# RWKV-7 head pairs 0 and 1 of a block side by side in one decoder block's kernel

## The chip, the cores and the metric

The kernel runs on one core of a Trainium2 chip. The core has a matrix engine (TensorE, PE in the profile; PEld are its weight loads), two engines for elementwise work (VectorE, DVE, and ScalarE, ACT), GpSimdE (POOL) and SyncE (SP), which only issues transfers here. ScalarE issues transfers too. Each engine works through its own instructions in the order in which they were laid out when the program was built, and waits on semaphores for the others. Matrix products land in PSUM (eight banks of 512 floats per partition); all else lies in SBUF or in DRAM. The metric is the time of one execution in microseconds (us) on the device.

## What is computed

One layer of a hybrid decoder, 2048 tokens of width 1024, all in 32-bit floats:

```python
h = rmsnorm(x, norm1_g) * (1.0 + sc1) + sh1
p = h @ w_in                       # 27 column groups of 128
ya = rglru_mixer(...)              # 256 wide
yb = hgrn2_mixer(...)              # 384 wide, 6 heads of 64
yc = rwkv7_mixer(...)              # 384 wide, 6 heads of 64
y = jnp.concatenate([ya, yb, yc], axis=-1) * mix_beta
x = x + g1 * (y @ w_out)
h = rmsnorm(x, norm2_g) * (1.0 + sc2) + sh2
x = x + g2 * swiglu(h, ffn_w_gate, ffn_w_up, ffn_w_down)
return rmsnorm(x, final_g)
```

The RWKV-7 mixer shifts each input column group by one token (`ps = pc + (prev - pc) * mu`), makes a decay `w` and a gate `a` per token from low-rank products (`tanh(wl) @ w_up`, `al @ a_up`, through a sigmoid) and an output gate `g = sigmoid(gl) @ g_up`, and runs this recurrence per head with a 64x64 state:

```python
sa = einsum('bhvk,bhk->bhv', S, -kkt)
S = S * wt + sa[..., None] * (kkt * at) + vt[..., None] * kt
y_t = einsum('bhvk,bhk->bhv', S, rt)
```

After it stand a group norm per head, a bonus term and the output gate.

## The kernel before

**Tiling.** Tokens are cut into 4 blocks of 512 (`TB`, `NB`), a block into 8 chunks of 64 (`NCH`). Channels lie on the 128 partitions, so an RWKV "pair" `pr` is two heads (`e` is 0 or 1), and there are three pairs.

**Dense work.** `project` (L238 to L249) multiplies weights, split into a rounded part and a rest (`wh`, `wl`), with activations split alike (`hh`, `hl`): three matmuls of 128x128 by 128x512 for each 128x128 weight block, 9696 in all. The raw weights come in through three buffers `wr`, and each is split by ScalarE (`wh`) and VectorE (`wl`, L221) into four buffers each.

**Order of work.** The program is written as straight Python and a planner orders the instructions of each engine by priority and by its own estimate of when operands are ready. `level` (L67) sets the priority: results of dense work first ("out"), then weight loads ("load"), norms and inputs ("feed"), the mixers ("mix"), and last the dense matmuls ("dense"). So dense matmuls fill TensorE wherever no mixer instruction was expected to be ready. `w_in_products` computes the 27 column groups of `p` in the order of `IN_ORDER` (L35), for blocks 0 and 1 together and then for 2 and 3, and stores them in DRAM (`pd`). `mixers(b)` reads them; its outputs go to `yd` in DRAM. `w_out_products` and `ffn` of block b are traced after `mixers(b + 1)`; `load_y` reads `yd` for the output projection.

**The mixers of a block** (L871): `lora`, then `rwkv` for pair 0, `hgrn` 0, `rglru` 0, `rwkv` for pairs 1 and 2, `hgrn` 1, `rglru` 1, `hgrn` 2.

`lora` (L473) keeps the low-rank inputs in the tiles `l1` and `l2` for the whole block. `rwkv` (L501) does one pair, in these stages:

- Prologue: two low-rank products (`low_rank`, L486) with a sigmoid give the decay input `sc` and the gate `a`; a scan along the tokens (L513), exponentials and products give per chunk the 128x256 operand `KG` and the 128x128 operand `BK`, with two buffers each. A matmul per chunk (L553), masked on VectorE (L556, L557), gives `GIQ`, one buffer, which holds the chunk's triangular system and its output weights. `BK` is transposed (L562).
- Inverse: the 32x32 diagonal blocks go through DRAM (`nd`, L569) into `NL` and `NX`, which lie with 32 blocks per group of 32 partitions, in four groups. 30 steps of a multiplication and an addition on VectorE (L599, L601) invert them. They go back through DRAM (`xd`, L607 and L610) into `GIQ`. Eight transposes of 32x32 per half (L617) and two rounds of eight 32x32 matmuls (L621, L626) make the off-diagonal blocks.
- Values: `v`, transposed and with its mean taken off, goes into `VS` (L584).
- Recurrence: for each of 8 chunks a chain of three visits to TensorE, with VectorE and ScalarE between: L641 (and L642), copy to `rs`; L650, copy to `VS`; L653 (and L654), then the new state with the decay `we` (L658). The products lie in one PSUM bank, `pc`.
- End: norm, bonus and output gate (L669), store to `yd` (L671).

A product of 32-bit operands shows as two instructions on TensorE, so 96 chunk steps (4 blocks, 3 pairs, 8 chunks) are x192 in the views. `hgrn` (L680) has its own tiles `VS2` and `AQ`. The scratch tiles of the RWKV part are nine buffers named `tr`, those of the other mixers eight named `th`. Tiles named `pm` are three PSUM banks, `ph` one, `pd` three, `pc` one.

Of the kernel before, what the change touches and what calls it, by code (L numbers as in the profile page):

```python
# [34 lines left out]
IN_ORDER = (25, 26, 19, 16, 22, 7, 4, 10, 13, 0, 2, 20, 17, 23, 8, 5, 11, 14, 1, 3, 21, 18, 24, 9, 6, 12, 15)  # L35
# [16 lines left out]
def hybrid_kernel(ctx, tc, x, par, ada_w, w_in, rgw, igw, w_up, a_up, g_up, w_out,  # L52
# [105 lines left out]
    ones = cp.tile([128, 128], F, name="ones")  # L158
    V.memset(ones, 1.0)
# [312 lines left out]

    def lora(b):  # L473
        t = shifted(b, 9, tr_())
        act(t[0:64], t[0:64], AF.Tanh)
        t1 = [mp.tile([128, TB], R, name=f"l1{i}", bufs=1) for i in range(2)]
# [4 lines left out]
        t2 = mp.tile([128, TB], F, name="l2", bufs=1)  # L481
        shifted(b, 10, t2)
        act(t2, t2, AF.Sigmoid)
        return t1, t2

    def low_rank(i, cols, l1):  # L486
        pz = pm_()
        PE.matmul(pz, LW[i][:, cols], l1[i], start=True, stop=False)
        PE.matmul(pz, LW[2 + i][:, cols], l1[i], start=False, stop=True)
        return pz  # L490
# [7 lines left out]
    GIQ = mp.tile([128, NCH, 2, 2, 64], F, name="GIQ")  # L498
    G.memset(GIQ, 0.0)

    def rwkv(b, pr, lr):  # L501
        cols = slice(pr * 128, (pr + 1) * 128)
        l1, l2 = lr
        k = shifted(b, 3 + pr, tr_())
        pz = low_rank(0, cols, l1)
        sc = tr65_()
        V.memset(sc[:, :, 0:1], 0.0)
        act(sc[:, :, 1:65], c64(pz), AF.Sigmoid, bias=pc("w0", pr))
        pz = low_rank(1, cols, l1)
        a = tr_()  # L510
        act(a, pz, AF.Sigmoid, bias=pc("a0", pr))
        cum = tr65_()
        V.tensor_tensor_scan(cum.rearrange("p c t -> p (c t)"), d0, sc.rearrange("p c t -> p (c t)"), 0.0,  # L513
                             op0=OP.mult, op1=OP.add)
# [28 lines left out]
        we = mp.tile([128, NCH], F, name="we", bufs=2)  # L543
# [5 lines left out]
        for q in range(0, NCH, 2):  # L549
# [4 lines left out]
            for e in range(2):  # L554
                s, o = HD[e]
                V.tensor_mul(GIQ[s, q:q + 2, :, e, :], pv[s, :, :, e], gm[s, None].to_broadcast([64, 2, 2, 64]))  # L556
# [7 lines left out]


        nd = tc.dram_tile([4 * NCH, 32, 32], F, name=f"nd{b}_{pr}")
        for blk in range(4):
            b2 = blk % 2
            A.dma_start(nd[blk * NCH:(blk + 1) * NCH].rearrange("c j i -> j c i"),  # L569
                         GIQ[32 * blk:32 * blk + 32, :, 0, blk // 2, 32 * b2:32 * b2 + 32])  # L570
        v = shifted(b, 6 + pr, tr_())
        pb, _ = blocksum(r, pm_(), "tr")
        VS = mp.tile([128, NCH, 2, 64], F, name="VS", bufs=1)
# [6 lines left out]
        for e in range(2):  # L580
            s, o = HD[e]
            for par in range(2):
                t = slice(par * 64, par * 64 + 64)
                stt(VS[o, par:NCH:2, e, :], mean[t, :, e:e + 1].to_broadcast([64, NG, 64]), -1.0 / 64, p4[t, :, e, :],  # L584
                    OP.mult, OP.add)
        bonus = v
        V.tensor_mul(bonus, v, pb)
        NL = mp.tile([128, 32, 32], F, name="NL", bufs=1)
        NX = mp.tile([128, 8, 32], F, name="NX", bufs=1)
        n4 = nd.rearrange("b (m g) i -> b m g i", g=4)  # L590
        for g in range(4):
            quarter = slice(32 * g, 32 * g + 32)
            A.dma_start(NL[quarter], nd)
            A.dma_start(NX[quarter], n4[:, :, g, :])
        for j in range(1, 31):
            m, n = (j + 3) // 4, 31 - j
            tmp = mp.tile([128, 72], F, name="ftmp", bufs=1)
            tv = tmp[:, :m * n].rearrange("p (c i) -> p c i", i=n)
# [3 lines left out]
        xd = tc.dram_tile([4 * NCH, 32, 32], F, name=f"xd{b}_{pr}")  # L602
        x4 = xd.rearrange("b (m g) i -> b m g i", g=4)
        for g in range(4):
# [428 lines left out]
```

## Time and profile before

| | |
|---|---|
| median of 3 runs | 2882.71 us (2879.23 to 2887.38) |
| the profiled execution, its own time | 2884.81 us |
| its span (first to last instruction) | 2883.0 us |
| TensorE's granted clock, mean | 0.986 |
| GpSimdE busy | 81.5 us |

A row of a group of instructions reads: line, engine, operation, tile written and tiles read, shape, count; then busy time and mean duration of one in ns; then the engine's idle time just before these instructions, and what ended it. Matmuls overlap each other in the pipeline, so a matmul's listed duration (399 ns for the dense ones) is longer than the distance from its start to the next one's. A row of the table of stretches reads: from and to, length; busy time and count of TensorE's matmuls, of its weight loads, of VectorE, ScalarE and GpSimdE; granted clock; share of the DMA engines, GB/s. A row of a timeline reads: start, duration, engine, line, operation; in brackets the engine's idle time before it and what ended it. A row of waits reads: who waited for whom, us in total, times, the longest. A DMA issue's row reads: shortest, median and longest time of the issue in ns, first and last start in us.

### The profile page before, as it was taken

The page shows a single profiled execution, that of the slowest core. Times are in us where ns is not written, and L with a number is a line of the kernel's source. Part 1 is how long each engine was busy: PE and PEld are TensorE (multiplying, and loading weights), DVE is VectorE, ACT ScalarE, POOL GpSimd, SP SyncE. Part 2 cuts the span into 40 slices and gives each one's busy share as a digit, 9 for nine tenths or more (in the row PEclk, how much of TensorE's full clock was granted, in tenths as well). Part 3 has the DMA queues.
Part 4 walks back from the last instruction along what each step waited for, and adds up shares of the span by engine and source line. Part 5 has one row for each costly group of instructions (what it writes and reads, how often), then busy time and mean ns, then how long its engine had stood idle before and what let it go on. Part 6 is the DMA issues. An engine that isn't in the chain of part 4 may idle for free. (4 is left out here: it accounts for less than half of the span.)

```text
span 2883.0 us, 41762 instructions
## 1 busy us (share of the span) xinstructions
PE 2761.2 (96%) x14842; PEld 2189.4 (76%) x14842; DVE 1975.3 (69%) x4617; ACT 1500.2 (52%) x2514; POOL 81.5 (3%) x67
## 2 busy tenths in 40 slices
PE   7999999999999899999989999999999999999998
PEld 6777777777777677777767787777777888788886
DVE  8776768778586777868788777778964444644445
ACT  4528465263636737565684556757644233533323
POOL 2000000000001000000100000001000001000000
PEclk9999999999999999999999999999999999999999
DMA  7534455434344233333453233344432333433332
GB/s 255 161 103 142 137 160 182 129 121 133 98 125 142 89 88 100 103 92 100 115 160 88 84 105 101 96 114 122 122 94 88 96 99 117 146 99 96 98 96 87
DMA packets 235041, 337.52 MB, mean 117 GB/s; under 512 B 73041, under 2 KB 78673, under 8 KB 234833
## 3 DMA queue, kind: packets, MB, share of 16 engines
q1 hardware_dynamic: 160144, 285.55, 31.9%
q10 hardware_dynamic: 74688, 49.31, 6.7%
q8 instruction: 117, 1.92, 0.3%
q14 instruction: 92, 0.75, 0.1%
HBM read 286.53 MB, written 48.23 MB: 116 GB/s over the span
## 5 line engine op out<-in xcount | busy, mean ns | idle before, releaser
L248 PE MATMUL pd<-hh,wh 128*128 128x512 f32 x3232 | 1285.4, 399 | 16.6 <-ACT hh L78 14.2
L248 PE MATMUL pd<-hl,wh 128*128 128x512 f32 x3232 | 1289.3, 399 | 3.1 <-DVE hl L81 3.0
L248 PE MATMUL pd<-hh,wl 128*128 128x512 f32 x3232 | 1283.6, 397 | 0.0
L78 ACT ACTIVATE wh<-wr 128x512 fp32r<-128x512 f32 (+1 forms) x752 | 463.6, 620 | 865.3 <-PE pd L248 713.4
L221 DVE TENSOR_TENSOR wl<-wr,wh 128x512 fp32r<-128x512 f32 (+1 forms) x752 | 509.0, 681 | 315.6 <-ACT wh L78 307.7
L248 PEld LDWEIGHTS pd<-hh,wh 128*128 128x128 f32 x3232 | 611.3, 189 | 144.0 <-ACT hh L78 17.7
L248 PEld LDWEIGHTS pd<-hl,wh 128*128 128x128 f32 x3232 | 611.8, 189 | 129.1 <-DVE hl L81 7.4
L248 PEld LDWEIGHTS pd<-hh,wl 128*128 128x128 f32 x3232 | 611.9, 189 | 121.9 <-issue 2.6
L81 DVE SCALAR_TENSOR_TENSOR xs<-pd,Q,xs 128x512 f32<-128x512 f32 x224 | 167.6, 748 | 124.6 <-PE pd L248 114.5
L78 ACT ACT_TABLE_LOAD x183 | 234.8, 1283 | 12.1 <-issue 4.7
L78 ACT ACTIVATE xs<-pd 128x512 f32<-128x512 f32 x140 | 82.8, 591 | 66.0 <-PE pd L248 60.8
L78 ACT ACTIVATE th<-th 128x512 f32<-128x512 f32 (+2 forms) x153 | 93.7, 613 | 44.9 <-DVE th L787 19.7
L917 DVE TENSOR_TENSOR xs<-pd,xs 128x512 f32<-128x512 f32 x88 | 60.7, 690 | 77.0 <-PE pd L248 75.2
L78 ACT ACTIVATE hh<-xs 128x512 fp32r<-128x512 f32 x120 | 74.1, 627 | 38.1 <-DVE xs L917 25.3
L78 ACT ACTIVATE hw<-VS,we 64x64 f32<-64x64 f32 x192 | 66.0, 344 | 42.2 <-DVE VS L81 38.8
L599 DVE TENSOR_TENSOR ftmp<-NX,NL 128x30 f32<-128x30 f32 (+4 forms) x360 | 73.9, 205 | 8.6 <-issue 1.2
L601 DVE TENSOR_TENSOR NX<-NX,ftmp 128x30 f32<-128x30 f32 (+4 forms) x360 | 73.7, 205 | 7.2
L78 ACT ACTIVATE tr<-tr 128x512 f32<-128x512 f32 (+3 forms) x100 | 62.3, 626 | 16.8 <-DVE tr L81 15.0
L81 DVE SCALAR_TENSOR_TENSOR VS<-pc,we,hw 64x64 f32<-64x64 f32 x168 | 47.4, 282 | 32.7 <-PE pc L653 28.9
L217 POOL TENSOR_TENSOR hl<-xs,hh 128x512 fp32r<-128x512 f32 x32 | 46.8, 1488 | 810.4 <-ACT hh L78 571.3
L78 ACT ACTIVATE xs<-xs 128x512 f32<-128x512 f32 x77 | 47.7, 626 | 36.1 <-DVE xs L81 22.9
L221 DVE TENSOR_TENSOR hl<-xs,hh 128x512 fp32r<-128x512 f32 x88 | 61.8, 703 | 5.6 <-ACT hh L78 1.1
(234 smaller groups left out, 2665.1 us busy)
## 6 DMA issues: line engine op xcount, KB each, us to landing
wr<-in_w_gate SPq DMA_DIRECT2D x176, 256.0 KB, 2.6
wr<-in_w_upf SPq DMA_DIRECT2D x176, 256.0 KB, 2.6
wr<-in_w_down SPq DMA_DIRECT2D x160, 256.0 KB, 2.7
wr<-in_w_in SPq DMA_DIRECT2D x144, 256.0 KB, 3.3
pd<-xs SPq DMA_DIRECT2D x108, 256.0 KB, 2.9
xs<-in_x SPq DMA_DIRECT2D x72, 256.0 KB, 4.4
wr<-in_ada_w SPq DMA_DIRECT2D x64, 256.0 KB, 3.3
th<-pd ACTq DMA_DIRECT2D x64, 256.0 KB, 3.4
```

What stands on the lines that cost most here:

```text
L78: return A.activation(o, i, f, **k)
L81: return V.scalar_tensor_tensor(o, a, s, b, op0=op0, op1=op1)
L217: G.tensor_sub(lo, src, hi.bitcast(F))
L221: V.tensor_sub(lo, src, hi.bitcast(F))
L248: PE.matmul(p, a[:, c], b, start=(n == 0), stop=(n == tot - 1))
L599: V.tensor_mul(tv, NX[:, 0:m, j:j + 1].to_broadcast([128, m, n]), NL[:, j:j + 1, j + 1:32].to_broadcast([128, m, n]))
L601: V.tensor_add(NX[:, 0:m, j + 1:32], NX[:, 0:m, j + 1:32], tv)
L917: V.tensor_mul(t, pu, t)
```

## The change

- `rwkv` takes a list of pairs. `mixers` calls it for pairs 0 and 1 together and then for pair 2 alone. `rwkv_chunks` (the prologue), `invert` and `rwkv_values` are functions of their own; `GIQ`, `VS`, `pc`, `rs` and `hw` have an index `u` for the pair within the call.
- `invert` puts the diagonal blocks of both pairs on the partitions: 64 blocks per group in two groups for a joint call, 32 in four for a single one. The 30 steps are the same, with about twice the elements per partition in a joint call. The 32x32 transposes of a half and pair are one instruction on 256 columns, and the matmuls of both halves come before the copies.
- In the recurrence each of the three visits does the products of both pairs; the copies to `rs` and `VS` serve both in one instruction. The decayed state (`hw`) and the new state are still one instruction per pair and head. The third visit's product overwrites the first's place in `pc`.
- `lora` computes the low-rank products of all three pairs at once and stores `sc`, `a` and the output gate's input in DRAM (`ld`); `rwkv_chunks` loads `sc` and `a`, and the end of `rwkv` loads the gate's input for each pair.
- Two tiles named `big` (2048 floats per partition) serve `NL`, `NX` and the scratch of the steps, then `VS`, and `VS2` with `AQ` of `hgrn`, in place of tiles of their own. `rs` and `hw` have one buffer instead of two, `we` four instead of two. `ones` is a view of `aones`.
- `IN_ORDER` brings the column groups of pair 1 forward.

```diff
-IN_ORDER = (25, 26, 19, 16, 22, 7, 4, 10, 13, 0, 2, 20, 17, 23, 8, 5, 11, 14, 1, 3, 21, 18, 24, 9, 6, 12, 15)
+IN_ORDER = (25, 26, 19, 16, 20, 17, 22, 23, 7, 4, 10, 13, 0, 2, 21, 18, 24, 8, 5, 11, 14, 1, 3, 9, 6, 12, 15)
...
     def lora(b):
...
+        ld = tc.dram_tile([4, 2, 128, 520], F, name=f"ld{b}")
+        t2 = shifted(b, 10, tr_())
         act(t2, t2, AF.Sigmoid)
+        A.dma_start(ld[3, 0, :, 0:TB], t2)
+        for pr in range(3):
+            cols = slice(pr * 128, (pr + 1) * 128)
+            pz = low_rank(0, cols, t1[0])
+            sc = tr65_()
+            V.memset(sc[:, :, 0:1], 0.0)
+            act(sc[:, :, 1:65], c64(pz), AF.Sigmoid, bias=pc("w0", pr))
+            A.dma_start(ld[pr, 0], sc.rearrange("p c t -> p (c t)"))
+            pz = low_rank(1, cols, t1[1])
+            a = tr_()
+            act(a, pz, AF.Sigmoid, bias=pc("a0", pr))
+            A.dma_start(ld[pr, 1, :, 0:TB], a)
+        return ld
...
+    def big_():
+        return mp.tile([128, 2048], F, name="big", bufs=2)
+
+    def rwkv_chunks(b, u, pr, ld, nd):
         k = shifted(b, 3 + pr, tr_())
+        sc = tile_of("tr")
+        A.dma_start(sc, ld[pr, 0])
         a = tr_()
-        act(a, pz, AF.Sigmoid, bias=pc("a0", pr))
+        A.dma_start(a, ld[pr, 1, :, 0:TB])
...
+    def invert(b, prs, nd):
+        nu = len(prs)
+        nb, ng = 4 * nu * NCH, 4 // nu
+        t = big_()
+        NL = t[:, 0:1024].rearrange("p (j i) -> p j i", i=32)
+        NX = t[:, 1024:1536].rearrange("p (m i) -> p m i", i=32)
+        n4 = nd.rearrange("b (m g) i -> b m g i", g=ng)
+        for g in range(ng):
+            part = slice(nb * g, nb * g + nb)
+            A.dma_start(NL[part], nd)
+            A.dma_start(NX[part, 0:32 // ng], n4[:, :, g, :])
         for j in range(1, 31):
-            m, n = (j + 3) // 4, 31 - j
+            m, n = (j + ng - 1) // ng, 31 - j
+            tv = t[:, 1536:1536 + m * n].rearrange("p (c i) -> p c i", i=n)
             V.tensor_mul(tv, NX[:, 0:m, j:j + 1].to_broadcast([128, m, n]),
                          NL[:, j:j + 1, j + 1:32].to_broadcast([128, m, n]))
             V.tensor_add(NX[:, 0:m, j + 1:32], NX[:, 0:m, j + 1:32], tv)
...
+        for e, (lo, up) in enumerate(half):
+            for u in range(nu):
+                V.transpose(X1[lo, u * 256:u * 256 + 256], GIQ[lo, :, u, 0, e, 0:32])
+            for u in range(nu):
+                for c in range(NCH):
+                    PE.matmul(pv[up, u, c], GIQ[lo, c, u, 0, e, 32:64], xv[lo, u, c], start=True, stop=True)
...
+    def rwkv(b, prs, ld):
+        nu = len(prs)
+        nd = tc.dram_tile([4 * nu * NCH, 32, 32], F, name=f"nd{b}_{prs[0]}")
+        ops = [rwkv_chunks(b, u, pr, ld, nd) for u, pr in enumerate(prs)]
+        invert(b, prs, nd)
+        VS = big_().rearrange("p (c u e v) -> p c u e v", u=2, e=2, v=64)
+        bonus = [rwkv_values(b, u, pr, op[3], VS) for u, (pr, op) in enumerate(zip(prs, ops))]
...
+                for u, (KG, BK, we, r) in enumerate(ops):
+                    PE.matmul(pcn[:, u, 0:2, :], KG[:, c, 0].rearrange("p e t -> p (e t)"), both[u], start=True, stop=True)
+                for u, (KG, BK, we, r) in enumerate(ops):
+                    PE.matmul(py[:, c - q, u], both[u], KG[:, c, 1], start=(c == q and u == 0), stop=False,
+                              skip_group_check=True)
+                V.tensor_copy(rs[0:64, 0:nu], pcn[0:64, 0:nu, 0, :])
+                act(rs[64:128, 0:nu], pcn[64:128, 0:nu, 1, :])
+                for u, (KG, BK, we, r) in enumerate(ops):
+                    for e in range(2):
+                        s, o = HD[e]
+                        act(hw[s, u], VS[s, c, u, e, :], AF.Copy, scale=we[s, c:c + 1])
+                for u in range(nu):
+                    PE.matmul(pcn[:, u, 2, :], GIQ[:, c, u, 0].rearrange("p e t -> p (e t)"), rs[:, u], start=True,
+                              stop=True)
+                V.tensor_copy(VS[0:64, c, 0:nu, 0, :], pcn[0:64, 0:nu, 2, :])
+                act(VS[64:128, c, 0:nu, 1, :], pcn[64:128, 0:nu, 2, :])
...
-            rwkv(b, 0, lr)
+            rwkv(b, (0, 1), lr)
             hgrn(b, 0)
             rglru(b, 0)
-            rwkv(b, 1, lr)
-            rwkv(b, 2, lr)
+            rwkv(b, (2,), lr)
```

More of the change, by code (lines that the diff above doesn't have):

```diff
@@ L157, in hybrid_kernel @@
     V.memset(aones.bitcast(F), 1.0)
-    ones = cp.tile([128, 128], F, name="ones")
-    V.memset(ones, 1.0)
+    ones = aones.bitcast(F)
     epsc = cp.tile([128, 3], F, name="epsc")
@@ L471, in shifted, with low_rank @@
         return t
+    def low_rank(i, cols, l1):
+        pz = pm_()
+        PE.matmul(pz, LW[i][:, cols], l1, start=True, stop=False)
+        PE.matmul(pz, LW[2 + i][:, cols], l1, start=False, stop=True)
+        return pz
     def lora(b):
@@ L475, in lora @@
         act(t[0:64], t[0:64], AF.Tanh)
-        t1 = [mp.tile([128, TB], R, name=f"l1{i}", bufs=1) for i in range(2)]
+        t1 = [tile_of("tr", R)[:, 0:TB] for i in range(2)]
         for i in range(2):
@@ L629, in rwkv @@
[L629 to L646 removed]
+        xd = tc.dram_tile([nb, 32, 32], F, name=f"xd{b}_{prs[0]}")
@@ new lines, in invert @@
+        x4 = xd.rearrange("b (m g) i -> b m g i", g=ng)
+        for g in range(ng):
+            part = slice(nb * g, nb * g + nb)
+            V.memset(NX[part].rearrange("p m i -> p (m i)")[:, g:1024 // ng:32 + ng], 1.0)
+            A.dma_start(x4[:, :, g, :], NX[part, 0:32 // ng])
+        for u in range(nu):
+            for blk in range(4):
+                b2 = blk % 2
+                n = (4 * u + blk) * NCH
+                A.dma_start(GIQ[32 * blk:32 * blk + 32, :, u, 0, blk // 2, 32 * b2:32 * b2 + 32],
+                            xd[n:n + NCH].rearrange("c l i -> l c i"))
@@ new lines, in invert @@
+        for e, (lo, up) in enumerate(half):
+            V.tensor_copy(TT[up, 0:n], p[up, 0:n])
+        p = pm_()
+        pv = p.rearrange("p (u c t) -> p u c t", u=2, t=32)
+        for e, (lo, up) in enumerate(half):
+            for u in range(nu):
+                for c in range(NCH):
+                    PE.matmul(pv[lo, u, c], tv[up, u, c], GIQ[up, c, u, 0, e, 32:64], start=True, stop=True)
+        for e, (lo, up) in enumerate(half):
+            for u in range(nu):
+                V.tensor_copy(GIQ[lo, :, u, 0, e, 32:64], pv[lo, u])
@@ L697, in hgrn @@
         pair = th_()[:, 0:TB // 2]
-        VS = mp.tile([128, 2, NCH, 64], F, name="VS2", bufs=1)
-        AQ = mp.tile([128, 2, NCH, 64], F, name="AQ", bufs=1)
+        VS, AQ = big_().rearrange("p (two e c v) -> two p e c v", two=2, e=2, v=64)
         p = ph_()
```

162 lines of the change are left out of this document (59 added, 103 removed).

## The prediction

> **What bounds the kernel now.** I read the page first (the span, part 1), then the table of stretches, the groups of TensorE by form, the DMAs that touch yd (the finished mixer outputs), the list of waits and two stretches of the timeline.
>
> ```profile
> span 2883.0 us, 41762 instructions
> ...
> PE 2761.2 (96%) x14842; PEld 2189.4 (76%) x14842; DVE 1975.3 (69%) x4617; ACT 1500.2 (52%) x2514; POOL 81.5 (3%) x67
> ```
>
> ```profile
> 2250.00:2400.00 150.00, 150.00 (x663) 124.27 (x662) 60.69 (x90) 45.73 (x75) 0.00 (x0) 1.00 0.33 98
> ```
>
> The first fence is the page's span and part 1, the second a stretch in which no mixer work is left: 663 dense matmuls in 150 us, 226 ns each, TensorE never idle.
>
> ```profile
> L248 PE MATMUL pd<-hl,wh 128*128 128x512 f32 x3232 | 1289.3, 399 | 3.1 <-DVE hl L81 3.0
> ...
> L641 PE MATMUL pc<-VS,KG 128*128 128x128 f32 x192 | 41.9, 300 | 4.1 <-DVE VS L81 3.9
> L653 PE MATMUL pc<-VS,BK 128*128 128x128 f32 x192 | 41.6, 298 | 5.5 <-ACT VS L78 5.0
> ...
> L650 PE MATMUL pc<-rs,GIQ 128*128 128x64 f32 x192 | 36.7, 273 | 3.5 <-ACT rs L78 3.3
> ...
> L621 PE MATMUL pm<-tr,GIQ 32*32 32x32 f32 x384 | 26.7, 199 | 4.4 <-DVE tr L617 4.1
> ```
>
> The dense product is issued in three kinds of 3232 instructions (one is quoted), 9696 in all: at 226 ns they need 2191 us of the 2883. The other 692 us hold 5146 small matmuls of the mixers and norms, the time lost in going over to them and back, and 122 us (2883.0 less 2761.2) of plain idle time. So TensorE is the bound, and only what shortens this remainder moves the end. Idle time in front of the recurrence (L641, L650, L653) is 13.1 us in all, in front of the inverse's matmuls (L621) 4.4 us: what stands idle openly is small.
>
> Is the mixers' chain a second bound? Source L671 stores a finished RWKV pair; L140 loads yd for the output projection of a block (here block 3; the answer for the tile yd in the window from 2100 us).
>
> ```profile
> L671 ACTq DMA_DIRECT2D yd<-tr x12: 326/326/353, 250.2 to 2199.0; - x12
> ```
>
> ```profile
> L140 SPq DMA_DIRECT2D xs<-yd x8: 319/327/435, 2414.7 to 2428.9; - x8
> ```
>
> The last RWKV output leaves at 2199.0 us and is asked for at 2414.7: 216 us to spare. The twelve stores are 11 intervals apart, (2199.0 - 250.2) / 11 = 177 us per pair, 531 us per block. Making this chain shorter gains nothing by itself; dense matmuls fill TensorE while it waits. What counts is how often TensorE must leave the dense stream for it.
>
> **The change part by part.**
>
> *Recurrence, pairs 0 and 1 together.* Every matmul is still issued (five products per pair and chunk), but a chunk step of two pairs has the three visits to TensorE (L641 with L642, L650, L653 with L654) that one pair had. Before: 4 blocks x 3 pairs x 8 chunks x 3 = 288 visits; after: 4 x 2 x 8 x 3 = 192, 96 fewer. The price of a visit beside its own matmuls:
>
> ```profile
> 1083.68 0.39 PE L248 MATMUL pd<-hh,wh 128*128 128x512 f32 x1
> 1083.91 0.38 PE L653 MATMUL pc<-VS,BK 128*128 128x128 f32 x2
> 1084.13 0.39 PE L654 MATMUL pm<-GIQ,VS 128*128 128x128 f32 x2
> 1084.27 0.48 PE L248 MATMUL pd<-hl,wh 128*128 128x512 f32 x1
> 1084.59 0.40 PE L248 MATMUL pd<-hh,wl 128*128 128x512 f32 x1
> ```
>
> Start to start, a dense matmul takes 0.23 us, but the first one after the visit takes 0.32 (1084.27 to 1084.59): 0.09 us on the way back. On the way in, the waits view gives what the weight loads waited:
>
> ```profile
> PEld pc L653 <- ACT VS L78: 20.8, 48, 1.8
> PEld pc L650 <- ACT rs L78: 19.7, 49, 1.0
> ...
> PEld pc L641 <- issue: 11.3, 32, 2.8
> ```
>
> That is 51.8 us over 288 visits, 0.18 us each at most; the matmuls' own idle rows above (13.1 us) make 0.045 at least, since a weight load can wait while the array still works. I take the middle, near 0.09, as half of each load wait lies under the dense matmul before it. A visit costs 0.09 + 0.09 = 0.18 us, and 96 fewer save **17 us**; ends 96 x 0.135 = 13 and 96 x 0.27 = 26 us. If the schedule puts dense matmuls between the two pairs' products, the visits do not shrink in number and the saving is near 0; that is the first rival.
>
> *Inverse, pairs 0 and 1 together.* Per pair, 16 transposes of 32x32 feed 16 products; now one 32x256 transpose per pair and half, and all products of both halves stand in one row.
>
> ```profile
> 1074.80 0.37 PE L621 MATMUL pm<-tr,GIQ 32*32 32x32 f32 x6
> 1075.10 0.50 PE L248 MATMUL pd<-hh,wl 128*128 128x512 f32 x1
> 1075.53 0.37 PE L621 MATMUL pm<-tr,GIQ 32*32 32x32 f32 x6
> ```
>
> The sixteen instructions of a half (two per product) come in pieces of six with one dense matmul between, which then holds TensorE for 0.43 us instead of 0.23 (1075.10 to 1075.53). The eight transposes of a half take 0.84 us; the view of line L621 says what ended its waits:
>
> ```profile
> 1074.03 0.84 DVE L617 STREAM_TRANSPOSE tr<-GIQ 32x32 f32<-32x32 f32 x8
> ```
>
> ```profile
>   DVE tr L617: 14.7, 19
>   issue: 10.6, 41
> ```
>
> 60 waits, 25.3 us, 0.42 each, over 12 pairs. After, 8 inversions with about two such entries each, 16 in all, at the transposes' own mean of 14.7 / 19 = 0.77 us since TensorE now waits for a whole transpose: 12.4 us. Saved: **13 us**. Ends: 25 if the order of issue foresees the wide transposes, 5 if each of the 24 (two per pair) keeps TensorE for the 0.84 us of eight narrow ones (20 us), and -8 if each of the 8 inversions meets a wait of 4.1 us, the whole wait in L621's row above (33 us): a wide transpose is not in this trace. I take the middle, nearest to the mean of L621's rows.
>
> *VectorE.* The substitution takes 60 instructions per inversion, 12 x 60 before and 8 x 60 after, with twice the elements for the joint ones.
>
> ```profile
> L601 DVE TENSOR_TENSOR NX<-NX,ftmp 128x60 f32<-128x60 f32 x48 | 10.4, 216 | 0.7
> ...
> L599 DVE TENSOR_TENSOR ftmp<-NX,NL 128x8 f32<-128x8 f32 x12 | 2.0, 166 | 0.3
> ```
>
> From 8 to 60 elements the time goes from 166 to 216 ns: 0.96 ns per element on 158. The sizes m x n average 47.5 elements with four groups and 86.7 with two, so 204 and 241 ns: 720 x 204 = 147 us before, 240 x 241 + 240 x 204 = 107 after, 40 us less. Shared copies of rs and VS in the recurrence and the transposes take perhaps 10 more. Worth 0 at the end: VectorE idles 31% of the span and TensorE does not wait for it but for the few us above. The cover is the dense stream; where it is gone (below) a faster VectorE helps.
>
> *Gates through DRAM, and the other DMAs.* Per block 7 stores and 9 loads are added (sc and a per pair, the gate input once stored and three times loaded), 64 issues on ScalarE's queue. Removed there: 5 x 48 = 240 issues of the inverse become 4 x 42 = 168.
>
> ```profile
> L461 ACTq DMA_DIRECT2D tr<-pd x44: 326/326/450, 64.2 to 2045.3; - x44
> ```
>
> ```profile
> L593 ACTq DMA_DIRECT2D NL<-nd x48: 308/608/1631, 129.5 to 2097.3; - x48
> L593 ACTq EVENT_SEMAPHORE  x24: 17/38/510, 129.4 to 2087.1; - x24
> ...
> DMA to landing us min/median/max: 2.0/2.7/6.3
> ```
>
> Net 8 issues fewer at 326 ns or more: nothing, and ScalarE is 48% idle. The new loads wait on stores, as NL's load of nd does; behind a waiting issue stand ScalarE's splits of the weights (wh), for which TensorE holds four tiles in hand. L593's 24 semaphore waits have a median of 38 ns and a maximum of 510, for the issue comes late enough; so I take 0. The bad end is 36 loads (sc, a and gate input of 12 pairs) x the 2.7 us of a landing = 97 us, less what the four tiles cover. One page speaks against this step: the Trainium skill, "DMA: Bandwidth & Descriptors", section "Anatomy of one DMA", says that DMA engines do not wait on semaphores and that any wait is held on the issuing sequencer before dispatch, so that ScalarE itself stands still. By that rule the sum would be nearer to its bad end; L593's waits do not bear it out here.
>
> *IN_ORDER, the shared ones, the sigmoids moved into lora, rs and hw with one buffer:* the same work at another place under dense matmuls; 0, with 5 us either way for the start, where the first chunk now waits for one more DRAM round trip.
>
> *The turn of each block* (norm before the FFN) keeps its stall, as nothing in the change feeds it; it may be filled more or less than now:
>
> ```profile
> 948.86 1.12 PE L299 MATMUL pd<-xs,ones 128*128 128x512 f32 x2 [2.57 <-DVE xs L281]
> 956.50 0.79 PE L257 MATMUL pm<-tr,bones 128*128 128x512 f32 x1 [6.52 <-ACT tr L78]
> ```
>
> About 9 us for this one, and a mixer matmul that happens to be ready there would use it. I take 0, with 10 us either way over all turns.
>
> **Sum.** 17 + 13 = 30 us against the profiled execution, 2884.8 us (span 2883.0 and 1.8 around it): 2855. It lies 2.1 us above the median of the runs, 2882.7, so the forecast is **2853 us**.
>
> **Rivals.**
>
> *No change (2875 to 2890, near 2880).* The pairs' products are pulled apart by dense matmuls, so visits stay near 288 and the wide transposes give back the inverse's gain. For it: TensorE's matmul count is the same, and open idle time before these lines is only 17.5 us. Against this rival: the visit price, in and out, is in the timeline whatever the idle rows say.
>
> *Slower: the mixers' chain becomes the bound.* Both KG and BK buffers belong to the joint pairs until their recurrence ends, and two "big" tiles serve the inverse, the RWKV values and HGRN2 together, which had their own. HGRN2 then cannot run beside the inverse, and pair 2 starts after the recurrence. The point: the chain now ends 216 us early, so a block must grow by more than 216 / 4 = 54 us, from 531 to over 585, before dense work runs out. From the first yd load of block 3 to the end are 2883.0 - 2414.7 = 468 us; a block of 600 us puts the last store at 2199 + 4 x 69 = 2475 and the end at 2943. Against it: two pairs one after the other are 354 us now, the joint steps are shorter, so a block should come out below 531 rather than above.
>
> *Slower: ScalarE stands behind the new loads.* If half of the 97 us gets through to TensorE, 2853 + 49 = 2902; it undoes the whole gain from a third on. For it: three loads per pair whose data were stored shortly before; against it: L593's short waits, and gates stored a block's prologue ahead of their use. The Trainium skill's page on DMA, cited above, stands on its side.
>
> *Faster still (2800 to 2840, near 2825).* Upper ends of both parts, 26 + 25, and some filled turns, 10: 61 us, 2822.
>
> **How the numbers follow.** Forecast (2840 to 2874) 0.48; faster still 0.19; no change 0.17; chain as bound 0.09; ScalarE behind loads 0.07. A measurement of this kernel tells about 0.3% (8.6 us) from no change. Faster by more than that: 0.48 + 0.19 and 0.02 of the third, 0.69. Within: 0.14 of the third and 0.02 of the last, 0.16. Slower: 0.09, 0.05 of the last and 0.01 of the third, 0.15. For 8 in 10 the range takes the forecast, most of the faster case and the no-change case: 2815 to 2892; the chain as bound lies outside.
>
> **What would show it.** Right: fewer and longer visits in the recurrence (six to eight instructions in a row instead of four), the inverse's small matmuls in runs of 16 or 32, the dense count and its 226 ns unchanged, VectorE down by some 50 us, the last yd store before 2199 us. Wrong: single dense matmuls between the two pairs' products; long waits of the inverse's matmuls for the transposes; idle TensorE ahead of the yd loads, with the last store after 2300 us; ScalarE waits ahead of wh ended by DMA; dense matmuls slower than 226 ns at a lower granted clock. If the time falls without fewer visits, my price of a visit was not the cause.

## The result, and the profile after

| | before | after |
|---|---|---|
| median of 4 runs each | 2882.88 us | 2917.63 us (2912.48 to 2921.73) |
| ratio, 95% interval | | 1.0119 (1.0096 to 1.0142) |
| the profiled execution | 2884.81 us | 2919.62 us |
| granted clock, mean | 0.986 | 0.975 |

The kernel became 35 us slower, 1.2%; the forecast was 2853 us, 30 us faster. The page of the kernel after:

```profile
span 2917.8 us, 41296 instructions
...
PE 2767.1 (95%) x14842; PEld 2213.5 (76%) x14842; DVE 1945.5 (67%) x4112; ACT 1480.5 (51%) x2472; POOL 86.1 (3%) x67
```

The same 14842 matmuls; VectorE has 505 instructions fewer and 30 us less to do, and TensorE is busy 6 us longer. The dense stream itself is as it was. The table of stretches, for 100 us without mixer work, gives 443 matmuls in 100 us, 226 ns each:

```profile
2300.00:2400.00 100.00, 100.00 (x443) 82.81 (x442) 43.25 (x64) 29.63 (x48) 0.00 (x0) 1.00 0.32 98
```

**Where the time is.** The same table by longer stretches, first of the kernel before, then of the kernel after:

```profile
0.00:900.00 900.00, 840.87 (x4827) 663.76 (x4828) 653.42 (x1681) 460.95 (x786) 33.62 (x31) 0.98 0.48 147
900.00:1500.00 600.00, 578.03 (x3233) 450.76 (x3232) 464.84 (x1127) 394.46 (x654) 19.40 (x16) 0.99 0.36 107
1500.00:2100.00 600.00, 579.16 (x3334) 452.47 (x3335) 479.86 (x1155) 364.71 (x609) 16.97 (x12) 0.99 0.36 104
```

```profile
0.00:900.00 900.00, 834.88 (x4625) 664.91 (x4625) 623.22 (x1408) 454.69 (x773) 32.57 (x29) 0.97 0.50 152
900.00:1500.00 600.00, 577.37 (x3222) 458.46 (x3222) 447.33 (x969) 352.17 (x581) 26.16 (x19) 0.98 0.38 112
1500.00:2100.00 600.00, 556.94 (x3102) 439.37 (x3103) 455.27 (x1023) 350.86 (x586) 15.87 (x12) 0.96 0.38 109
```

Look at 1500 to 2100 us. Before, TensorE was idle there for 600 - 579 = 21 us at a clock of 0.99; after, for 43 us at 0.96. Both kernels work on the same things there: the end of block 1's turn, the dense work of the FFN, the mixers of blocks 2 and 3, and block 2's turn. In the other two stretches idle time hardly moved (59 to 65 us, 22 to 23).

What TensorE waited for, in the waits of the kernel before and of the kernel after:

```profile
PE pd L248 <- ACT hh L78: 14.2, 5, 5.9
...
PE pc L653 <- ACT VS L78: 5.0, 8, 1.4
...
PE pc L641 <- DVE VS L81: 3.9, 4, 2.4
PE ph L257 <- ACT th L78: 3.8, 3, 3.3
...
PE ph L816 <- DVE th L81: 2.4, 4, 0.9
```

```profile
PE pd L247 <- ACT hh L78: 27.1, 8, 4.5
PE ph L256 <- ACT th L78: 14.7, 8, 6.1
...
PE ph L867 <- DVE th L81: 12.9, 4, 6.6
PE pm L564 <- DVE KG L553: 8.1, 5, 5.4
PE pm L643 <- DVE tr L640: 8.0, 6, 3.4
```

Of the recurrence's own waits (L653, L641 and L650, 12.2 us) 5.0 are left, 4.4 of them at the second visit (L692, before L650). In their place stand few and long ones: dense products behind the splits of their activations (hh), and two products of the mixers, the sums over a head's channels (L256, before L257) behind ScalarE and the RG-LRU tile's product (L867, before L816) behind VectorE. The last one waits 12.9 us in 4 pieces, before 2.4 us in 4.

**What a long wait costs.** The timeline of the kernel after, at the end of block 2's turn:

```profile
2048.18 0.40 PE L247 MATMUL pd<-hh,wl 128*128 128x512 f32 x1
2053.54 0.80 PE L247 MATMUL pd<-hh,wh 128*128 128x512 f32 x1 [4.96 <-DVE xs L81]
2054.13 0.63 PE L247 MATMUL pd<-hl,wh 128*128 128x512 f32 x1
...
2057.89 0.39 PE L247 MATMUL pd<-hl,wh 128*128 128x512 f32 x1
```

VectorE's operation that ended this wait had itself waited for a load of the turn's next tile `xs`:

```profile
2052.74 0.75 DVE L81 SCALAR_TENSOR_TENSOR xs<-pd,Q,xs 128x512 f32<-128x512 f32 x1 [1.99 <-DMA xs<-in_x]
```

The table of stretches around the wait:

```profile
2047.50:2050.90 3.40, 1.08 (x5) 0.56 (x3) 2.77 (x6) 0.67 (x2) 0.00 (x0) 1.00 0.77 231
2050.90:2057.80 6.90, 4.26 (x10) 3.43 (x11) 3.28 (x5) 0.63 (x1) 0.00 (x0) 0.51 0.77 239
2057.80:2064.70 6.90, 6.90 (x31) 5.67 (x31) 4.39 (x14) 3.02 (x7) 0.00 (x0) 1.00 0.69 202
```

TensorE stands idle for 4.96 us. While it does, the granted clock falls to half, and the first nine matmuls behind it come 0.43 us apart instead of 0.23: some 1.8 us more.

**The whole sum.** With the clock's records one can split each span. "Warm work" is the time with a matmul running, less half of what of it lies in stretches at half clock; that half is the next column. "Long stalls" are idle stretches of 2 us and more. A "visit" is a run of TensorE instructions between two dense ones. "In the turns" is how much of the half clock and of all idle time lies in the 150 us from the first load of yd of each block, the four blocks together (in the kernel after they begin at 886.9, 1399.1, 1951.5 and 2449.0 us). All are counted in the traces; the runs e3 to e14 are those below. The execution of e12 that was profiled (2883.7 us) is the slowest of its seven.

| kernel | span us | visits | warm work us | half clock, while busy us | long stalls, us (number) | shorter stalls us | in the turns us |
|---|---|---|---|---|---|---|---|
| before | 2883.0 | 680 | 2732.7 | 28.6 | 43.5 (13) | 52.4 | 58.7 |
| after | 2917.8 | 514 | 2717.8 | 49.3 | 79.7 (21) | 45.7 | 95.6 |
| e3, old column order | 2880.6 | 536 | 2716.4 | 31.5 | 53.4 (15) | 53.7 | 67.6 |
| e5, columns three places later | 2902.5 | 517 | 2715.7 | 43.2 | 76.4 (21) | 41.8 | 89.8 |
| e10, pair 2 first | 2881.8 | 576 | 2720.1 | 31.2 | 39.0 (11) | 65.8 | 60.6 |
| e12, late column order | 2881.9 | 531 | 2711.2 | 45.2 | 55.6 (15) | 44.8 | 67.8 |
| e7, before with shared tiles | 2919.4 | 634 | 2737.4 | 49.7 | 54.6 (14) | 52.5 | 85.6 |
| e8, before with gates in DRAM | 2898.5 | 692 | 2739.2 | 33.9 | 43.6 (11) | 56.0 | 61.5 |
| e11, before with new columns | 2897.8 | 664 | 2737.8 | 40.4 | 36.3 (9) | 57.9 | 54.4 |
| e14, late order, pair 2 first | 2976.4 | 559 | 2718.7 | 66.6 | 112.1 (25) | 53.3 | 149.5 |

The change does what it says: 166 visits and 15 us of warm work fewer, 7 us less in short stalls. It gives back 36 us in long stalls and 21 us in half clock. -15 - 7 + 36 + 21 = 35 (the rest, the start and the end, is 25 to 26 us in both).

The loss has a place: idle time and half clock in the turns grew from 59 us to 96, by 37. In all ten kernels with joint pairs the warm work is 2710 to 2720 us and what is lost outside the turns 92 to 108 us; what differs is the turns. Spans of 2876 to 2882 us go with 61 to 68 us lost there (e3, e6, e10, e12), 2892 to 2894 with 76 (e2, e9), 2902 with 90 (e5), 2912 with 104 (e15), 2918 with 96 (the changed kernel) and 2976 with 149 (e14).

### The profile page after: what moved, and what is told of

Its sections match the earlier page's. It is cut to its first block, busy times and chain, and to the rows that moved or that the text cites. A ratio compares the mean times of both kernels' runs of the same rounds, so it can differ in the third digit from the quotient of the medians.

```text
span 2917.8 us, 41296 instructions
## 1 busy us (share of the span) xinstructions
PE 2767.1 (95%) x14842; PEld 2213.5 (76%) x14842; DVE 1945.5 (67%) x4112; ACT 1480.5 (51%) x2472; POOL 86.1 (3%) x67
## 5 line engine op out<-in xcount | busy, mean ns | idle before, releaser
L247 PE MATMUL pd<-hh,wh 128*128 128x512 f32 x3232 | 1288.4, 399 | 33.5 <-ACT hh L78 27.1
L78 ACT ACTIVATE hw<-big,we 64x64 f32<-64x64 f32 x192 | 66.2, 345 | 52.1 <-DVE big L81 45.9
L78 ACT ACTIVATE tr<-tr 128x512 fp32r<-128x512 f32 (+4 forms) x112 | 69.5, 627 | 10.6 <-DVE tr L81 4.7
L539 POOL MEMSET KG<- 64x1024 f32 x24 | 22.7, 946 | 1701.0 <-PE pc L679 839.0
L81 DVE SCALAR_TENSOR_TENSOR big<-pc,we,hw 64x64 f32<-64x64 f32 x168 | 47.6, 283 | 24.7 <-PE pc L697 21.6
L564 PE MATMUL pm<-KG,BK 128*128 128x256 f32 x192 | 50.5, 409 | 11.7 <-DVE KG L553 8.1
```

What stands on the lines that cost most here:

```text
L78: return A.activation(o, i, f, **k)
L81: return V.scalar_tensor_tensor(o, a, s, b, op0=op0, op1=op1)
L247: PE.matmul(p, a[:, c], b, start=(n == 0), stop=(n == tot - 1))
L539: G.memset(KG[o, :, :, e], 0.0)
L564: PE.matmul(ps[:, (c - q) * 256:(c - q + 1) * 256], BK[:, c, :], KG[:, c], start=True, stop=True)
```

## The experiments

Three theories. *Placing:* the new instructions are cheaper, but they meet the dense stream at worse places; then another order of the same work gives the loss back. *Price of a part:* the shared "big" tiles or the gates in DRAM cost time wherever they stand. *The turn*, a narrow form of placing: pair 2's inverse falls on the turns of the blocks. The names in the expectations changed as the runs came in; each explains its own. Unless told otherwise a run is one execution, beside one of the kernel before on the same chip. Seven executions of one kernel (e12) lay between 2867 and 2884 us and twelve of the kernel before between 2875 and 2891, so single executions of one kernel were up to 17 us apart, and a smaller difference between two single ones says little.

### e1 and e2: HGRN2 pair 0 and RG-LRU tile 0 exchanged, before and after

```diff
-            hgrn(b, 0)
             rglru(b, 0)
+            hgrn(b, 0)
```

> The kernel before, with HGRN2 0 and RG-LRU 0 traced in the other order; every instruction is the same, only the planner's order can differ. Theory A (the loss of 35 us belongs to the joint pairs and what comes with them): this stays within 9 us of 2883, with about four idle stretches of TensorE over 3.4 us. Theory B (any re-laying of the order moves a few long stalls, and with them the time): it moves by more than 9 us one way or the other, with the number of idle stretches over 3.4 us moving along.

> The changed kernel with the same exchange of HGRN2 0 and RG-LRU 0. Theory A: within 9 us of 2918, with about thirteen idle stretches over 3.4 us. Theory B: it moves by more than 9 us either way, and the long stalls stand at other places.

The kernel before became 2895.6 us (2878.6 beside it, +17); the changed one 2893.9, +15 over the kernel before, where it had been +34 (1.19% of 2878.6). So an exchange that has nothing to do with the change takes about half of its loss away; what it does to the kernel before is as wide as the scatter, no more.

### e3: the changed kernel with the old order of columns

```diff
-IN_ORDER = (25, 26, 19, 16, 20, 17, 22, 23, 7, 4, 10, 13, 0, 2, 21, 18, 24, 8, 5, 11, 14, 1, 3, 9, 6, 12, 15)
+IN_ORDER = (25, 26, 19, 16, 22, 7, 4, 10, 13, 0, 2, 20, 17, 23, 8, 5, 11, 14, 1, 3, 21, 18, 24, 9, 6, 12, 15)
```

> The changed kernel with the order of the input columns of before. If the new IN_ORDER brings the loss, this comes near 2885. Theory A: 2918 or slower, since pair 1 then starts later, and the difference lies before 500 us. Theory B: anywhere from 2880 to 2950.

2882.4 us (2878.6 beside it), +4 instead of +34. The stretch that had lost, in its table of stretches:

```profile
1500.00:2100.00 600.00, 580.86 (x3262) 463.94 (x3261) 456.19 (x993) 375.75 (x614) 14.65 (x12) 0.99 0.38 113
```

19 us of idle time at 0.99, as in the kernel before. The warm work stays at 2716. Everything else of the change is still there, so about 30 of the 35 us belong to the order of the columns in this kernel, and the joint pairs by themselves are not what lost them.

### e4: the changed kernel with three single calls

```diff
-            rwkv(b, (0, 1), lr)
+            rwkv(b, (0,), lr)
...
-            rwkv(b, (2,), lr)
+            rwkv(b, (1,), lr)
+            rwkv(b, (2,), lr)
```

> The changed code with every pair alone (three calls of one pair, in the places of before): gates through DRAM, shared tiles, wide transposes and the new column order stay, side by side goes. If the joint steps bring the loss: near 2883 or below. If the gates through DRAM or the shared tiles bring it: 2910 or more. My forecast's own logic (a visit costs 0.18 us) makes it 17 us slower than the changed kernel, 2935.

3000.6 us (2878.6), the slowest of all. The last output of the mixers leaves at 2555.4 us, while block 3's output projection begins to load at 2456.6; TensorE then stands idle for 12.5 us in one piece. So with shared tiles, gates in DRAM and the new order of columns single pairs make the mixers' chain the bound, and the joint form saves some 88 us (3000.6 against 1.0119 x 2878.6 = 2913). The joint pairs pay for the room that they take.

### e5, e6 and e12: pair 1's columns three and ten places later

```diff
-IN_ORDER = (25, 26, 19, 16, 20, 17, 22, 23, 7, 4, 10, 13, 0, 2, 21, 18, 24, 8, 5, 11, 14, 1, 3, 9, 6, 12, 15)
+IN_ORDER = (25, 26, 19, 16, 22, 7, 4, 20, 17, 23, 10, 13, 0, 2, 21, 18, 24, 8, 5, 11, 14, 1, 3, 9, 6, 12, 15)
...
+IN_ORDER = (25, 26, 19, 16, 22, 7, 4, 10, 13, 0, 2, 8, 5, 11, 20, 17, 23, 21, 18, 24, 14, 1, 3, 9, 6, 12, 15)
```

> The changed kernel, with the columns of pair 1 (20, 17, 23) three places later than in the change; nothing else. The runs so far put TensorE's own work (busy time less what a lowered clock costs) at 2717 us in every joint kernel and 2733 in the kernels of before, so the difference lies in long stalls. Theory P (phase: in the changed kernel the inverse of pair 2 falls on every turn of a block, near 957, 1510 and 2073 us, because both recur every 560 us): the mixers move about 25 us later, partly off the turns: 2890 to 2905. Theory B (any order draws its stalls anew): own work 2717 again, time anywhere from 2875 to 2930.

> The changed kernel with the columns of pair 1 ten places later; the mixers of block 0 start their joint part some 80 us later. Theory P: the inverses of pair 2 stand clear of the turns (near 1020, 1590 and 2140 us), so about 2882 as with the old column order, although work starts later. Theory B: own work 2717, time anywhere from 2875 to 2930. If the chain were the bound: 2918 + 80.

> The changed kernel with the columns of pair 1 ten places later, timed against the kernel before. One look gave 2877.8 against 2878.6. The change's own gain on TensorE is about 15 us of warm work and 7 us of short waits, and what is left of the long stalls and the half clock behind them gives that back: ratio 0.997 to 1.003. A ratio below 0.997 would mean that this version beats both kernels; above 1.003, that the look was a lucky one.

e5: 2904.3 us (2878.6 beside it); pair 2's substitution still ran on the turns (1495 to 1531, 2052 to 2091). e6: 2877.8 (2878.6); it ran at 1610 to 1632 and 2177 to 2197, well off them. e12, the same kernel as e6 in 7 executions on another chip against 12 of the kernel before: median 2873.43 against 2882.84, ratio **0.9959 (0.9944 to 0.9973)**. This version beats both kernels. The table of stretches and the waits of e12:

```profile
1500.00:2100.00 600.00, 584.24 (x3302) 466.76 (x3301) 449.21 (x976) 370.38 (x613) 21.58 (x16) 0.99 0.38 113
```

```profile
PE pd L247 <- ACT hh L78: 24.5, 7, 6.7
...
PE ph L256 <- ACT th L78: 7.7, 4, 4.6
...
PE ph L867 <- DVE th L81: 2.2, 2, 1.3
```

Only 16 us idle from 1500 to 2100 at 0.99. The RG-LRU product waits 2.2 us instead of 12.9, and the sums at L256 7.7 instead of 14.7; the waits for hh are nearly those of the changed kernel (27.1).

### e7 and e13: the kernel before with the shared tiles, in two orders

```diff
-        VS = mp.tile([128, NCH, 2, 64], F, name="VS", bufs=1)
+        VS = big_()[:, 0:1024].rearrange("p (c e v) -> p c e v", e=2, v=64)
...
-        NL = mp.tile([128, 32, 32], F, name="NL", bufs=1)
-        NX = mp.tile([128, 8, 32], F, name="NX", bufs=1)
+        bt = big_()
+        NL = bt[:, 0:1024].rearrange("p (j i) -> p j i", i=32)
+        NX = bt[:, 1024:1280].rearrange("p (m i) -> p m i", i=32)
...
-        VS = mp.tile([128, 2, NCH, 64], F, name="VS2", bufs=1)
-        AQ = mp.tile([128, 2, NCH, 64], F, name="AQ", bufs=1)
+        VS, AQ = big_().rearrange("p (two e c v) -> two p e c v", two=2, e=2, v=64)
```

> The kernel before with only its large tiles shared (NL, NX, VS and HGRN2's two tiles out of two buffers). If the shared tiles made the single-pair form of the change slow (3001 us): the mixers' chain grows from 531 us a block to about 600 and the time goes to 2950 to 3000. If not: within 20 us of 2883. TensorE's own work stays at 2733 either way.

> The kernel before with the two shared tiles, and HGRN2 pair 0 and RG-LRU tile 0 exchanged. The shared tiles alone gave 2921 (e7), the exchange alone 2896 (e1), the kernel before 2879. If sharing has a price of its own (work that must wait for the tile), it adds about 40 us to the exchanged kernel too: 2925 to 2945. If e7's 40 us came from where its stalls happened to fall (stalls over 2 us and the half clock behind them, which made 32 of the 36 us of its span), another order of the calls draws other stalls: 2878 to 2915.

e7: 2921.2 us (2878.6 beside it, +43). e13, with the exchange of e1 on top: 2947.1 (2888.2, +59, where the exchange alone had given +17). The tiles add about 42 us in both orders, far over the scatter: they have a price of their own while the pairs run singly. How they get it can be read from the last outputs. e7's last store to yd, from HGRN2, and block 3's loads:

```profile
L799 ACTq DMA_DIRECT2D yd<-th x12: 326/327/391, 252.3 to 2448.7; - x12
```

```profile
L140 SPq DMA_DIRECT2D xs<-yd x8: 319/327/427, 2451.1 to 2465.2; - x8
```

Where the kernel before had 216 us to spare, 2.4 are left: a block's mixers recur every 579 us instead of 520 (last store of block 0 to last of block 3, over three). TensorE is not yet starved by it, and only 11 of the 36 us that its span is longer are long stalls; 21 are half clock. 27 of the 36 us lie in the turns (59 us before, 86 here); why the slower mixers cost time just there was not taken apart further.

### e8: the kernel before with the gates through DRAM

```diff
-        l1, l2 = lr
+        ld = lr
...
-        pz = low_rank(0, cols, l1)
...
-        pz = low_rank(1, cols, l1)
+        sc = tile_of("tr")
+        A.dma_start(sc, ld[pr, 0])
         a = tr_()
-        act(a, pz, AF.Sigmoid, bias=pc("a0", pr))
+        A.dma_start(a, ld[pr, 1, :, 0:TB])
```

with the changed kernel's `lora`.

> The kernel before with only the gates computed for all pairs at the start of a block, stored in DRAM and loaded back. If the gates made the single-pair form slow: 2930 or more, with the chain at 600 us a block. My forecast's term for this edit was 0: within 20 us of 2883, own work 2733.

2900.3 us (2878.6, +22). The long stalls are what they were (43.6 us), and the loads are hardly waited for: all instructions that wait for `ld` in its trace wait 8.4 us together, 0.3 of it on TensorE (its weight load for the output gate). Its span is 15.5 us above that of the profiled execution of before: 6.5 us of warm work, 5 of half clock, 4 of short stalls. The exchange of e1, which changes no instruction, brought nearly as much (+17), so it stays open whether this is a price of the loads.

### e9 and e10: pair 2 one mixer later, and directly behind the joint pairs

```diff
             rwkv(b, (0, 1), lr)
             hgrn(b, 0)
             rglru(b, 0)
-            rwkv(b, (2,), lr)
             hgrn(b, 1)
+            rwkv(b, (2,), lr)
```

(e9; in e10 the call stands ahead of `hgrn(b, 0)`.)

> The changed kernel with pair 2 of each block one mixer later (HGRN2 pair 1 ahead of it); same instructions, same order of the w_in columns. Theory P (pair 2's inverse, whose substitution ran at 942-982, 1507-1545 and 2062-2098 us, sits on the turns at about 957, 1510 and 2073): the substitution moves some 50 to 90 us later, off the turns; the idle time and the lost clock in the four turns together fall from 109 us to 85 or less, and the time is 2875 to 2893. Theory B (each order of the work draws its stalls anew, the inverse has nothing special): the time lies anywhere in 2878 to 2921, as e1 to e8 did, and the turns lose about as much with the inverse beside them as without. A time above 2900 with the substitution off the turns speaks against P.

> The changed kernel with pair 2 of each block directly behind the joint pairs (ahead of HGRN2 pair 0 and the RG-LRU tile 0). Theory P: its inverse moves some 100 us earlier, to about 840, 1400 and 1960 us, off the turns at 957, 1510 and 2073, and the time is 2875 to 2893, unless HGRN2 and the RG-LRU tile that then fall on the turns stall them as well. Theory B: anywhere in 2878 to 2921. If the turns lose 100 us or more together with no inverse beside them, P in its narrow form is wrong: then it is any in-order VectorE work there that does it.

e9: 2895.3 us; e10: 2883.6 (2882.84 median beside them). Neither moved as expected: pair 2's substitution still ran at 1497 to 1539 and 2053 to 2097 in e9, at 1502 to 1521 and 2062 to 2081 in e10. In e10 the turns with the inverse still on them lost little: idle time and half clock in the four turns, as in the table above, are 61 us together, 59 in the kernel before, 96 in the changed one and 76 in e9 (the expectation's 109 is a slightly different count of the same). So the narrow theory of the turn falls: an inverse on the turn is not enough for the loss. Placing in general stands: e10 is the changed kernel with one call moved, and it stands 1 us above the kernel before instead of 34.

### e11: the kernel before with the new order of columns

The diff of `IN_ORDER` is the change's own.

> The kernel before with the changed kernel's order of the w_in columns, nothing else. If that order is bad by itself (the columns of pair 1, three places each, are early and those of HGRN2 later), the time is 2895 to 2915, since giving the old order back took 35 us off the changed kernel. If the order only shifts the mixers against the turns, the kernel before, whose period is 531 us, is moved to another phase and shows 2875 to 2895. Under theory B anywhere in 2878 to 2900.

2899.6 us (median of 2882.84 beside it, +17): barely outside the scatter of single executions, within the expectation for an order that is bad by itself. But its loss is not the one of the changed kernel: that one lies in the turns, and here the turns take 54 us, against 59 in the kernel before. As far as one execution shows, the order costs the turns only together with the rest of the change.

### e14 and e15: both mends at once

e14 has e12's column order and e10's order of calls; e15 e3's columns and e10's calls.

> The changed kernel with both edits that gave back its loss: the late order of the columns (e12, 0.996 of before) and pair 2 directly behind the joint pairs (e10, 2884). Warm work of TensorE stays at 2710 to 2722 us. If the two edits remove different stalls, 2850 to 2868. If stalls are drawn anew by any order, 2870 to 2900.

> The changed kernel with the order of the columns of before (e3, 2882) and pair 2 directly behind the joint pairs (e10, 2884). If the two edits remove different stalls, 2850 to 2870. If stalls are drawn anew by any order, 2870 to 2900.

e14: 2978.2 us (2888.2 beside it, +90). e15: 2913.6 (+25). Neither theory had this. In e14's trace, the stores to yd by HGRN2, block 3's loads, and TensorE's timeline behind them:

```profile
L848 ACTq DMA_DIRECT2D yd<-th x12: 326/326/344, 624.2 to 2532.9; - x12
```

```profile
L140 SPq DMA_DIRECT2D xs<-yd x8: 320/400/426, 2462.7 to 2536.7; - x8
```

```profile
2539.05 0.79 PE L247 MATMUL pd<-hh,wh 128*128 128x512 f32 x1 [12.35 <-ACT hh L78]
```

The loads of block 3 begin at 2462.7 but the last has to wait for a store at 2532.9: dense work runs out, and TensorE idles 12.35 us in one piece. e15 runs out in the same way: its loads of block 3 begin at 2402.1, its last store is at 2468.9, and TensorE idles 12.51 us in one piece behind it. The mends do not add up because both move the mixers back: later columns start them later, and with pair 2 ahead of HGRN2 the last outputs come later. The changed kernel's last store is at 2288.8, its first load of block 3 at 2449.0, a slack of 160 us; in e12 it is 18 us (2395.8 to 2413.9), in e10 31 (2381.9 to 2412.5), and with both edits there is none. So the two orders decide on two losses: the stalls at the turns, and the slack of the chain.

## Why the prediction was wrong

**The bound and the visits: right.** TensorE is the bound and its dense stream did not change. I had 96 fewer visits of the recurrence; counted are 115 (281 to 166, those with L642 or its like L681 alone left out). The timeline of the kernel after shows the longer ones:

```profile
258.86 0.39 PE L247 MATMUL pd<-hh,wl 128*128 128x512 f32 x1
259.09 0.55 PE L692 MATMUL pc<-rs,GIQ 128*128 128x64 f32 x4
259.45 0.48 PE L247 MATMUL pd<-hh,wh 128*128 128x512 f32 x1
...
260.93 0.67 PE L697 MATMUL pc<-big,BK 128*128 128x128 f32 x4
261.43 0.61 PE L699 MATMUL pm<-GIQ,big 128*128 128x128 f32 x4
```

Four L692 of both pairs in one visit, and eight in the next, with no dense matmul between the pairs. Of the 64 joint and single chunk steps only 4 have their first products (L679) in two visits, and none those of L692 or L697. The rival "no change" had its ground in pairs pulled apart, and did not occur.

**The two terms of the sum: right in kind, too large, and one for a wrong reason.** I had 17 us for the recurrence and 13 for the inverse, 30 us. Measured are 15 us of warm work and, in this order of the work, 7 of short stalls: 22 us for 166 visits of all kinds, 0.13 us each. That average lies near the lower bound of my price, 0.135, and not at 0.18. Only the warm work is firm: it is 2710 to 2720 us in the ten kernels with joint pairs and 2733 to 2739 in the six that keep the single pairs of before, while the short stalls of the joint ones lie anywhere from 38 to 66 us (52 in the kernel before). The two terms were not measured apart. e4, single pairs with all else of the change, has 2723 us of warm work, which would leave the smaller part to the joint steps; but there dense work runs out, so it is no clean measure.

For the inverse, the waits at L621 (25.3 us, weight loads and matmuls together) were to become 12.4. The same view of the kernel after, line L643, says

```profile
  DVE tr L640: 19.7, 15
  issue: 3.8, 10
```

23.5 us, hardly less: a wait for a wide transpose is 1.3 us in the mean, where I had put the 0.77 of the narrow ones, although the wide transpose itself takes 434 ns in the median and eight narrow ones took 840. What fell is the number of visits with a matmul of the inverse, from 90 to 28, which I had not counted.

**VectorE: right for the substitution.** That was to fall from 147 us to 107; it fell from 147.5 in 720 instructions to 109.3 in 480. All of VectorE's work fell by 30 us, where I had some 50. I gave it no worth, and no run tells its worth apart.

**The gates: not refuted.** I took 0, with a bad end that the Trainium skill's page "DMA: Bandwidth & Descriptors", section "Anatomy of one DMA", spoke for. In the kernel after, VectorE is the only engine that waits for the loaded gates,

```profile
  DVE tr L525: 1.5, 1
```

1.5 us once. On ScalarE's queue three semaphore waits of 17 ns each stand ahead of the 36 loads, and no wait of ScalarE is ended by one of these transfers: half of 97 us did not get through. e8's +22 us stands against the 0, but not with waits for these loads.

**The step that failed** is the pair of zeros. For the order of the columns and the work that moved I had "the same work at another place under dense matmuls; 0, with 5 us either way"; for the turn of each block, that it "keeps its stall, as nothing in the change feeds it", and "I take 0, with 10 us either way over all turns". The turns took 37 us more (59 to 96): 26 of idle time and 11 of half clock. Over the whole span long stalls grew by 36 us, and half clock by 21, which I had not priced at all: my terms counted idle time at its face value. The first zero holds only where dense matmuls cover the work, and at a turn they run out; the second forgot that the turn's own work goes through the same queues, in order, as the mixers' work that the change moves.

The waits of the turns are of several kinds. The turn's bare stall shows at block 3, where no mixer work is left: 4.26 us until hh, in the kernels before and after alike. On top of it, dense products wait longer for hh, 27.1 us in all against 14.2. Then a mixer's matmul has a fixed place among the dense ones, so when its operand is later than planned, everything behind it on TensorE waits too: L256 and L867. And transfers of the turn's own tiles come late, as at 2052.74 above. One wait separates most of the slow runs from the others: VectorE and ScalarE wait for stores of finished `xs` tiles to the output, in the kernel after

```profile
ACT xs L78 <- DMA out<-xs: 12.1, 3, 5.7
```

and 4.2 us more on VectorE. These waits come to 16.3 us in the changed kernel, 10.8 in e5, 10.3 in e9, 6.7 in e7 and 12.4 in e13; there are none in the other twelve traces, with those of before, e3, e10 and e12 among them. But e2 has none either and loses 76 us in its turns, and no run gives `xs` more buffers, so this is a lead and not a cause shown.

e3 shows the place: with the old columns the stretch from 1500 to 2100 us loses 19 us instead of 43, the turns 68 instead of 96, and 30 of the 35 us are gone. So that the order of the work draws these stalls is shown by e3, e10 and e12; which instruction collides with which is not settled, and the one collision that I named (e9, e10) was not it.

**The chain as the bound: right in its point, and nearer than I thought.** I set the point at a block of over 585 us and gave it 0.09. From the last store of block 0 to that of block 3, a block's mixers take 520 us in the kernel before and 533 in the changed one, not less than before as I had argued; the last store is at 2288.8 us, where I had put it before 2199. With 160 us of slack left, this rival did not decide. But the shared tiles that I named as its cause do lengthen the chain (e7: 579 us, 2.4 us of slack), and single pairs with all else of the change pass the point (e4: 603 us a block). My estimate for 600 us was an end at 2943; e4 took 3000.6, as its last store came at 2555 and not at 2475: already block 0's last output was 107 us later than before (745 against 638). That the joint form is shorter than two pairs one after the other, my argument against this rival, is borne out by the 533 us against e4's 603.

## What to carry to other kernels

A kernel whose matrix engine is filled by a planner has two costs that busy time doesn't show: stalls long enough to lower the clock, and the slack of the side chain. Before costing a reordering at nothing, look at the few places where the filler runs out (here the turns, where 37 us were lost), list what will stand in the in-order queues there, transfers included, and price each new stall with the half clock behind it. When a structural change loses, try its parts and a few orders of the unchanged work before giving it up: here the joint pairs with another order of columns are 0.4% faster than the kernel before, and with the order that they came with 1.2% slower.

## What the hardware showed

**Two microseconds of idle time in one window are enough for half clock.** In all 17 traces the granted clock changes on a grid of 3.41 us. Counted over them, the first 60 us and the end left out: of the 182 windows in which TensorE ran at full clock and was idle for 2.0 us or more, all 182 were followed by a window at half clock; of 97 with 1.5 to 2.0 us 41 were, of some 13,150 with less 24. At half clock an idle time of 0.5 us and more kept the next window at half in 246 of 251 cases. The stretch from 2047.5 to 2050.9 us above is one of the 182: 2.3 us idle, and half clock from 2050.9. So two stalls of equal length can differ in price by where they lie on the grid, and a stall right behind another prolongs the slow time. The Trainium skill's page "TensorE: Matmul & The Clock Gate", section "What's actually happening", gives the same window, 3413 ns and free-running, and the same half rate; the rule of its section "Why this matters for your kernels", to have no idle gaps over about 3 us, is too lax for these traces.

**VectorE's splits are slower while GpSimdE works.** In the kernel after, from 1405 to 1420 us GpSimdE is busy for 10.0 us; VectorE's five splits `wl` between 1405 and 1425 took 925 ns in the mean, the 752 of the whole span 684:

```profile
L220 DVE TENSOR_TENSOR wl<-wr,wh 128x512 fp32r<-128x512 f32 x5 | 4.6, 925 | 0.0
```

```profile
L220 DVE TENSOR_TENSOR wl<-wr,wh 128x512 fp32r<-128x512 f32 (+1 forms) x752 | 511.6, 684 | 321.3 <-ACT wh L78 314.3
```

GpSimdE works there on the splits `hl` of the next output projection, which is at a turn. Over the whole trace the 16 of 720 splits `wl` of this shape that overlap GpSimdE's work took 1098 ns in the mean, and none of the other 704 took over 695. The kernel before shows the same (20 splits, 910 ns; the others at most 695), so this is no loss of the change by itself. But of the 12.9 us that TensorE waits at L867, 10.0 are two waits (3.47 us until 1417, 6.56 until 1978) in stretches where GpSimdE does these splits; that its work is why VectorE was late there is likely and was not tested.
